# Output projection in two parts: groups B and C multiplied beside group A's attention and parked in DRAM, groups A and D after it

## The chip, the cores and the metric

The kernel runs on one core of one Trainium2 chip. The metric is the device time of one launch in microseconds, as the median of several runs. Lower is better. One further execution was recorded by the hardware profiler; the rows below come from it.

## The reference, cut to what matters

Two layers over 512 latent tokens and 256 context tokens, width 1024, float32. In each layer four head groups (A windowed attention, B convolution, C differential attention, D neighbourhood attention) each produce 256 of the 1024 channels. Their concatenation is multiplied by one matrix, gated and added to the stream; a normalisation that is scaled and shifted by the conditioning vector, and a feed-forward network, follow.

```python
y_a = window_gqa(qa, ka, va, ka_c, va_c, sink)
y_b = conformer_conv(ub, conv_w, conv_b, conv_ln_g, conv_ln_b)
y_c = diff_out(diff_attention_latent(qc, kc, vc, kc_c, vc_c, lam), subln_g, lambda_init)
y_d = neighbourhood_attn(qd, kd, vd, kd_c, vd_c, rpb)
yx = jnp.concatenate([y_a, y_b, y_c, y_d], axis=-1) @ w_out
...
x = x + g1 * yx
x = x + g2 * swiglu(modulate(rmsnorm(x, norm2_g[l]), sh2, sc2), w_gate[l], w_up[l], w_down[l])
```

The product can be cut along the channels: `[B C] @ w_out[256:768] + [A D] @ (the other 512 rows)` is the same sum. In the first layer the context tokens pass through the same steps; in the second only the latent tokens do.

## The kernel before, in words

Tokens are handled in row tiles of 128: tiles 0 to 3 are latent, 4 and 5 context. Layer 0 has six tiles, layer 1 four. Every float32 product of a weight and an activation is made of three matmuls on rounded parts (`mm3`, lines 174 to 179: high by high, high by low, low by high), so each operand is first split into a high part by ScalarE (line 142) and a low part by VectorE (line 144). Group outputs lie transposed in four tiles `yA` to `yD` (`self.yg`), two blocks of 128 channels each.

A layer (`layer`, line 995) is a sequence of stages. Inside a stage two generators run abreast: `beside(main, side, nm, ns)` (line 928) takes `ns` steps of the side work for every `nm` steps of the main work, which sets the order in which instructions are written down. A compile-time list scheduler takes that order as priority: on each engine, the earliest-written instruction that its model of the chip has ready goes next. After compilation the order on each engine and on SP's DMA queue is fixed, and each of them waits in order.

The stages around the change:

- Group D's second half, `beside(self.d_attn(l, ..., 1), rest(), dn, ...)` (line 1134). `rest` (line 1110) finishes group A's input projection, frees the input `hT`, opens the pool `wo` for the output weights, and runs `c_norm` (line 678), which normalises group C's output in pairs of row tiles through the PSUM tag `pu`.
- Group A's attention (line 1138): `a_attn` for two heads at a time, four query blocks each, and in layer 0 `ctx_attn` for the context tokens. Each block makes scores in the PSUM tag `sc`, a softmax on VectorE, ScalarE and GpSimd, transposes through `pt` (`tr_copy`, line 508), and the product with the values through `pu` (`pv`, line 616). Its side work is `more` (line 1119): it loads and splits output weights (`load_wo`, line 957; blocks 0 to 5 of 8 in layer 0, 0 and 1 in layer 1) and in layer 0 computes modulation vector 2 (`ada_gen`, `ada_half`, lines 335 and 298).
- The output projection (from line 1146). It reloads `x` (lines 1150 to 1155), loads the remaining output weights, loads and splits the first three feed-forward weights ahead, loads the gate `g1`, and then, row tile by row tile (context tiles first), splits the four groups into `yh` and `yl`, makes 8 blocks x 2 halves x 3 = 48 matmuls, and calls `add_gated` (line 981: one product `gt` from PSUM, line 984, and one sum into `x`, line 987) and for the first tiles `norm_rows` (line 362). In layer 0 modulation vector 4 is computed between the tiles: eight loads of 512 KB through `wraw` (3 buffers) and `araw` (1 buffer) in turn (`ada_load`, line 284), each followed by its matmuls (line 311), and a transpose per half (line 326). The second normalisation's scale is that vector. Before the last row tile's last blocks, `norm_mod` (line 394) transposes and modulates the first pair of normalised tiles; the feed-forward matmuls read its result.

PSUM has eight banks of 512 floats. Modes are pushed and popped as a stack (`PSUM_TAGS`, line 75): `t` holds `pt` (2 banks), `u` holds `pu` (2), and above them lies `c` (`sc`, 4 banks) or, in group D's stage, `e` (`sd` 2, `ptd` 2). So in group A's stage `sc` stands where `sd` and `ptd` stood, and `pu` keeps its banks.

## Time and profile before

| | |
|---|---|
| median of 3 runs | 1773.85 us (1773.67 to 1779.73) |
| the profiled execution's own time | 1774.57 us |
| its span, first to last instruction | 1772.7 us |
| TensorE matmul (PE) busy | 1701.2 us, 96% |
| weight load (PEld) busy, overlaps PE | 1412.6 us, 80% |
| VectorE (DVE), ScalarE (ACT), GpSimd (POOL) busy | 933.1, 583.3, 209.1 us |
| DMA | 172.78 MB, mean 97 GB/s |
| the chain that ended last | PE 84%, DVE 5%, DMA 4%, ACT 2% |

A row of a timeline gives start, duration, engine, line, operation, what it writes and reads, and in brackets the idle time of the engine before it and what ended that. A row of a windows view gives the length of a stretch, each engine's busy time with its instruction count, the clock granted to TensorE as a share of full speed, the share of time that the DMA engines were busy, and their GB/s. Matmuls are pipelined, so the distance between two starts, not the duration of one, is what a matmul costs.

### The profile page before, as it was taken

How to read it: one execution, taken by the hardware profiler on the slowest of the kernel's cores; microseconds unless marked ns; L12 is line 12 of the kernel's file. 1: busy time of each engine (PE TensorE's matmuls, PEld its weight loads, DVE VectorE, ACT ScalarE, POOL GpSimd, SP SyncE). 2: the span in 40 equal slices, each digit the busy share in tenths (PEclk: the TensorE clock that was granted, in tenths of full speed). 3: DMA queues.
4: the chain of work that ended last, by engine and by line, in shares of the span. 5: the costliest groups of instructions: out<-in, count | busy, mean ns of one | idle time of the engine just before them, and what ended most of it. 6: DMA issues, size and time to landing. Idle time of an engine off the chain costs nothing.

```text
span 1772.7 us, 27001 instructions
## 1 busy us (share of the span) xinstructions
PE 1701.2 (96%) x11236; PEld 1412.6 (80%) x11236; DVE 933.1 (53%) x1548; ACT 583.3 (33%) x1048; POOL 209.1 (12%) x194
## 2 busy tenths in 40 slices
PE   6999998889999999999999999999999999999997
PEld 4888777667888888888888888878767888888886
DVE  4678885663442343332333358688566545354354
ACT  4225553562241112121121224455365422321221
POOL 1101124330000010000000010112341001000000
PEclk8999999999999999999999999999999999999999
DMA  9351121325066344243221222211105253432421
GB/s 326 81 170 37 37 55 41 102 89 202 26 186 201 109 134 144 74 144 97 60 73 47 84 72 60 60 39 42 33 25 179 81 170 96 119 94 73 119 72 48
DMA packets 187976, 172.78 MB, mean 97 GB/s; under 512 B 17878, under 2 KB 150478, under 8 KB 187726
## 3 DMA queue, kind: packets, MB, share of 16 engines
q1 hardware_dynamic: 187854, 171.06, 31.6%
q8 instruction: 88, 1.44, 0.3%
q14 instruction: 34, 0.28, 0.0%
HBM read 166.76 MB, written 4.52 MB: 97 GB/s over the span
## 4 chain that ended last, share of the span: by engine, by line
PE 84%; DVE 5%; DMA 4%; ACT 2%; issue 1%; SPq 1%; POOL 1%; POOLq 0%; DVEq 0%; ACTq 0%
PE ps L177 19%; PE ps L178 19%; PE ps L179 19%; PE pu L177 5%; PE pu L178 5%; PE pu L179 4%; PE sc L630 3%; PE pt L515 3%; PE pt L621 2%; PE ada L311 2%; DMA wraw<-in_w_in 1%; SPq L98 1%; PE pu L621 1%; DMA x<-in_x 1%; DVE PT L529 1%
## 5 line engine op out<-in xcount | busy, mean ns | idle before, releaser
L178 PE MATMUL ps<-h,whi 128*128 128x512 f32 (+1 forms) x1104 | 382.8, 347 | 2.5 <-DVE h L144 2.5
L177 PE MATMUL ps<-h,whi 128*128 128x512 f32 (+1 forms) x1104 | 382.4, 349 | 0.9 <-DVE gt L984 0.9
L179 PE MATMUL ps<-h,wlo 128*128 128x512 f32 (+1 forms) x1104 | 381.6, 346 | 0.0
L142 ACT CAST whi<-wraw 128x1024 fp32r<-128x1024 f32 (+1 forms) x132 | 134.4, 1022 | 452.5 <-PE ps L178 248.8
L144 DVE TENSOR_TENSOR wlo<-wraw,whi 128x1024 fp32r<-128x1024 f32 (+1 forms) x116 | 137.7, 1190 | 193.5 <-ACT whi L142 192.4
L178 PEld LDWEIGHTS ps<-h,whi 128*128 128x128 f32 x1104 | 209.0, 189 | 29.1 <-DVE h L144 3.2
L177 PEld LDWEIGHTS ps<-h,whi 128*128 128x128 f32 x1104 | 207.8, 189 | 30.0 <-issue 2.4
L179 PEld LDWEIGHTS ps<-h,wlo 128*128 128x128 f32 x1104 | 208.9, 189 | 26.2 <-issue 0.4
L177 PE MATMUL ps<-wdhi,zh 128*128 128x512 f32 x440 | 171.6, 392 | 0.4 <-ACT ntmp L386 0.4
L178 PE MATMUL ps<-wdlo,zh 128*128 128x512 f32 x440 | 171.2, 390 | 0.0
L179 PE MATMUL ps<-wdhi,zl 128*128 128x512 f32 x440 | 170.6, 391 | 0.0
L177 PE MATMUL pu<-hT,whi 128*128 128x512 f32 (+1 forms) x456 | 161.1, 354 | 4.9 <-DVE V L910 3.8
L178 PE MATMUL pu<-hT,whi 128*128 128x512 f32 (+1 forms) x456 | 160.3, 352 | 0.0
L179 PE MATMUL pu<-hT,wlo 128*128 128x512 f32 (+1 forms) x456 | 159.7, 350 | 0.5 <-DVE wlo L144 0.5
L984 DVE TENSOR_TENSOR gt<-ps,g 128x1024 f32<-128x1024 f32 x66 | 80.7, 1223 | 134.2 <-PE ps L179 128.0
L142 ACT CAST wdhi<-wraw 128x1024 fp32r<-128x1024 f32 x44 | 46.1, 1052 | 272.6 <-PE ps L179 182.3
L987 POOL TENSOR_TENSOR x<-x,gt 128x1024 f32<-128x1024 f32 x12 | 29.7, 2474 | 728.7 <-DVE gt L984 728.7
L1250 DVE TENSOR_TENSOR sg<-sg,ps 128x768 f32<-128x768 f32 (+1 forms) x44 | 36.1, 821 | 145.8 <-PE ps L179 144.3
L879 DVE SCALAR_TENSOR_TENSOR accd<-hp,wcol,accd 128x783 f32<-128x783 f32 (+1 forms) x116 | 107.8, 929 | 2.7 <-ACT accd L875 1.2
L177 PEld LDWEIGHTS pu<-hT,whi 128*128 128x128 f32 x456 | 86.4, 190 | 20.2 <-DVE V L910 4.2
L177 PEld LDWEIGHTS ps<-wdhi,zh 128*128 128x128 f32 x440 | 82.6, 188 | 18.9 <-issue 1.0
L179 PEld LDWEIGHTS ps<-wdhi,zl 128*128 128x128 f32 x440 | 82.6, 188 | 17.8 <-issue 0.6
(260 smaller groups left out, 2712.3 us busy)
## 6 DMA issues: line engine op xcount, KB each, us to landing
araw<-in_w_ada SPq DMA_DIRECT2D x68, 512.0 KB
wraw<-in_w_gate SPq DMA_DIRECT2D x44, 512.0 KB
wraw<-in_w_up SPq DMA_DIRECT2D x44, 512.0 KB
wraw<-in_w_down SPq DMA_DIRECT2D x44, 512.0 KB
wraw<-in_w_in SPq DMA_DIRECT2D x40, 512.0 KB
wraw<-in_w_ada SPq DMA_DIRECT2D x17, 512.0 KB
wraw<-in_w_out SPq DMA_DIRECT2D x12, 512.0 KB
x<-in_x SPq DMA_DIRECT2D x8, 512.0 KB
```

The lines of the kernel that those rows point to most:

```text
L142: nc.scalar.copy(hi, src)
L144: eng.tensor_tensor(lo, src, f32(hi), op=ALU.subtract)
L177: mm(out, st[0], mv[0], start=first, stop=False)
L178: mm(out, st[0], mv[1], start=False, stop=False)
L179: mm(out, st[1], mv[0], start=False, stop=last)
L311: nc.tensor.matmul(ps[32 * j:32 * j + 32, 0:P], self.cstat[:, k, :], raw[:, a * 512 + j * P:a * 512 + (j + 1) * P], start=(k == 0), stop=( ...
L515: self.nc.tensor.transpose(pt[:, (i - a) * P:(i - a + 1) * P], blocks[i], self.ident)
L621: self.burst_of([lambda i=i, j=j: nc.tensor.matmul(po[64 * j:64 * j + 64, 0:P], *parts[j][i], start=(i == n - 1), stop=(i == 0)) for i in ...
L630: return [lambda o=o, q=q[a][r], k=k[b][r], i=i: self.nc.tensor.matmul(o, q, k, start=(i == 0), stop=(i == 2)) for i, (a, b) in enumerate( ...
L879: nc.vector.scalar_tensor_tensor(acc[:, 0:w], hp[:, k:k + w], wc, acc[:, 0:w], op0=ALU.mult, op1=ALU.add)
L984: nc.vector.tensor_tensor(tmp, ps, g, op=ALU.mult)
L1250: nc.vector.tensor_tensor(sg, sg, pss[1][:, 0:W], op=ALU.mult)
```

## The change

The four channel blocks 2 to 5 (groups B and C) of each row tile are multiplied in group A's stage, by a new generator `out_part`, copied from PSUM by ScalarE into an SBUF tile, and written to a DRAM tile `opark`. The later projection multiplies blocks 0, 1, 6, 7 only, loads the parked tile into `part`, and VectorE adds it before `add_gated`. Weight blocks 2 to 5 are loaded in `rest`, blocks 0 and 1 in `more`, blocks 6 and 7 afterwards, in both layers. Group A's stage gets a PSUM mode of its own, `a`: `sc` with 4 banks, `pu` with one and `pq` with one (the new product's, and the modulation's); mode `u` is popped for it, so `sc` now covers the two banks of the old `pu` and those of `sd`. The steps of side work per main work are changed with it, and in `norm_mod`'s place the condition `k == wa` becomes `k == 2` of four blocks.

```diff
+        "a": {"sc": (2048, 1), "pu": (512, 1), "pq": (512, 1)},
...
+        self.opark = self.tl(self.drp, [6, P, D], "opark")
...
+    def out_part(self, l, wo, pool, c2, order):
+
+        for n, i in enumerate(order):
+            yh, yl = (self.tl(pool, [P, 512], "rt", 4).bitcast(F32R).rearrange("p (k t) -> p k t", k=4) for _ in range(2))
+            for gi, gn in enumerate("BC"):
+                self.split(yh[:, 2 * gi:2 * gi + 2, :], yl[:, 2 * gi:2 * gi + 2, :], self.yg[gn][:, :, i * P:(i + 1) * P])
+            y = self.tl(pool, [P, 6, 256], "V", 1) if n % 2 else self.tl(c2, [P, 6, 256], "VD", 1)
+            y = y.rearrange("p a c -> p (a c)")[:, 0:D]
+            for hf in range(2):
+                c = slice(hf * 512, hf * 512 + 512)
+                ps = self.ps("pq")
+                for k in range(2, 6):
+                    self.mm3(ps, (yh[:, k - 2, :], yl[:, k - 2, :]), (wo[k][0][:, c], wo[k][1][:, c]), k == 2, k == 5)
+                nc = self.nc
+                nc.scalar.copy(y[:, c], ps)
+                if hf:
+                    self.dma(self.opark[i], y)
+                yield
...
             yield from self.c_norm(l, c1)
+            yield from self.load_wo(l, wo, held["wop"], range(2, 6))
 
         def more():
-            self.burst, self.ada_tag = 15, ("pu", "pt")[l]
+            self.burst, self.ada_tag = 15, "pq"
             self.atags = [("wraw", 3, F32, self.wst), ("whi", 3, F32R, self.wst), ("wlo", 3, F32R, self.wst)]
-            yield from self.load_wo(l, wo, held["wop"], range(wa))
+            yield from self.out_part(l, wo, c1, held["c2"], tiles)
+            yield from self.load_wo(l, wo, held["wop"], range(2))
             yield from self.ada_gen([] if l else [(0, 2)])
...
-        self.beside(self.d_attn(l, held["c2"], 1), rest(), dn, 4 if cx else 3)
+        self.beside(self.d_attn(l, held["c2"], 1), rest(), dn, 8 if cx else 7)
         self.psum_pop()
-        self.psum_push("c")
+        self.psum_pop()
+        self.psum_push("a")
         self.pv_tag = "pu"
-        self.beside(self.chain(self.a_attn(l, 0), self.a_attn(l, 1)), more(), 2 * dn, (12, 3)[l])
+        prs = order if cx else order[1:]
+        tiles = [i for pr in prs for i in pr]
+        self.beside(self.chain(self.a_attn(l, 0), self.a_attn(l, 1)), more(), 2 * dn, (16, 10)[l])
...
-        for _ in self.load_wo(l, wo, wop2, range(wa, NK)):
+        for _ in self.load_wo(l, wo, wop2, range(6, NK)):
...
-                yh = self.tl(op, [P, NK, P], "yh", 2, F32R)
-                yl = self.tl(op, [P, NK, P], "yl", 2, F32R)
-                for gi, gn in enumerate("ABCD"):
+                yh = self.tl(op, [P, 4, P], "yh", 2, F32R)
+                yl = self.tl(op, [P, 4, P], "yl", 2, F32R)
+                part = self.tl(op, [P, D], "part", 2)
+                self.dma(part, self.opark[i])
+                for gi, gn in enumerate("AD"):
...
-                for k in range(NK):
-                    if i == 3 and k == wa:
+                for k in range(4):
+                    if i == 3 and k == 2:
...
-                self.add_gated(xs[i], ps, g1[int(i >= 4)], op)
+                nc.vector.tensor_tensor(part, ps, part, op=ALU.add)
+                self.add_gated(xs[i], part, g1[int(i >= 4)], op)
```

## Rows read from the trace of the kernel before

**Rows 1.** The page, busy time of each engine and its share of the span

```profile
PE 1701.2 (96%) x11236; PEld 1412.6 (80%) x11236; DVE 933.1 (53%) x1548; ACT 583.3 (33%) x1048; POOL 209.1 (12%) x194
```

**Rows 2.** Windows, layer 0: group A's stage, its parts, and the output projection

```profile
345.00:402.00 57.00, 48.21 (x547) 36.51 (x543) 35.75 (x107) 35.40 (x96) 20.68 (x17) 0.94 0.27 86
...
360.00:380.00 20.00, 19.32 (x262) 14.77 (x262) 11.90 (x42) 10.58 (x34) 5.71 (x6) 1.00 0.16 55
380.00:390.00 10.00, 6.19 (x76) 4.76 (x76) 5.52 (x15) 5.63 (x12) 3.64 (x4) 1.00 0.29 82
390.00:402.00 12.00, 10.38 (x85) 7.41 (x85) 8.47 (x18) 8.02 (x25) 1.84 (x1) 0.72 0.77 246
...
402.00:474.00 72.00, 71.91 (x419) 58.30 (x418) 25.76 (x49) 13.04 (x33) 1.66 (x3) 1.00 0.38 127
```

**Rows 3.** Windows, layer 1: group A's stage, and the output projection

```profile
1302.00:1345.00 43.00, 38.36 (x364) 28.82 (x362) 27.00 (x82) 29.00 (x71) 20.22 (x18) 0.96 0.14 46
1345.00:1391.00 46.00, 45.44 (x207) 37.49 (x208) 22.78 (x37) 15.49 (x32) 1.66 (x3) 1.00 0.51 160
```

**Rows 4.** PE's timeline in layer 0's projection: two matmuls, 48 apart

```profile
404.05 0.39 PE L179 MATMUL ps<-wohi,yl 128*128 128x512 f32 x1
...
414.93 0.39 PE L179 MATMUL ps<-wohi,yl 128*128 128x512 f32 x1
```

**Rows 5.** PE's timeline at the end of layer 0's group A stage

```profile
384.59 0.98 PE L630 MATMUL sc<-qk,qk 64*128 64x256 f32 x12
388.75 0.63 PE L515 MATMUL pt<-ident,Pm 128*128 128x128 f32 x4 [3.19 <-DVE r L820]
...
393.62 2.39 PE L621 MATMUL pu<-PT,VA 128*64 128x128 f32 x18 [1.05 <-ACT PT L526]
```

**Rows 6.** DVE's timeline at the end of layer 1's group A stage

```profile
1335.99 3.81 DVE L144 TENSOR_TENSOR wolo<-wraw,wohi 128x1024 fp32r<-128x1024 f32 x3
```

**Rows 7.** ACT's copy of 512 columns from PSUM, in its timeline

```profile
398.11 0.59 ACT L526 COPY PT<-pt 128x512 f32<-128x512 f32 x1 [1.16 <-PE pt L515]
```

**Rows 8.** PE's timeline, layer 0: group C's norm and group A's first scores

```profile
324.29 0.60 PE L689 MATMUL pu<-ident,yC 128*128 128x128 f32 x4
...
345.45 0.96 PE L630 MATMUL sc<-qk,qk 64*128 64x256 f32 x12
...
353.37 0.66 PE L707 MATMUL pu<-ident,rt 128*128 128x128 f32 x4 [0.58 <-DVE rt L701]
```

**Rows 9.** PE's timeline, layer 0's projection: modulation vector 4, first modulated pair, first feed-forward matmuls

```profile
420.46 0.65 PE L311 MATMUL ada<-araw,cstat 128*32 128x128 f32 x16
...
443.14 0.64 PE L311 MATMUL ada<-araw,cstat 128*32 128x128 f32 x16
448.66 0.27 PE L326 MATMUL ada<-ident,adab 128*128 128x128 f32 x1
...
469.68 1.03 PE L381 MATMUL ada<-ident,xn 128*128 128x128 f32 x8
...
474.08 0.48 PE L177 MATMUL ps<-h,whi 128*128 128x256 f32 x2
```

**Rows 10.** SP's timeline, layer 0's projection: loads of the single buffer araw

```profile
407.08 0.75 SPq L98 DMA_DIRECT2D araw<-in_w_ada  x1
...
435.53 0.52 SPq L98 DMA_DIRECT2D araw<-in_w_ada  x1
```

**Rows 11.** Windows: the DMA engines as layer 0's projection begins

```profile
395.00:413.00 18.00, 17.77 (x116) 13.81 (x113) 6.25 (x19) 6.37 (x20) 0.00 (x0) 0.94 0.86 298
```

**Rows 12.** Tiles gt and yl, with DVE's timeline for xn: VectorE's durations in the projection

```profile
L984 DVE TENSOR_TENSOR gt<-ps,g x66: 1204/1225/1227, 415.6 to 1697.4; 128x1024 f32<-128x1024 f32 x66
L987 DVE TENSOR_TENSOR x<-x,gt x54: 1215/1225/2172, 416.9 to 1698.6; 128x1024 f32<-128x1024 f32 x54
...
L144 DVE TENSOR_TENSOR yl<-yA,yh x10: 416/418/426, 402.1 to 1369.1; 128x256 fp32r<-128x256 f32 x10
...
1363.48 0.75 DVE L368 TENSOR_SCALAR xn<-x,rs 128x1024 f32<-128x1024 f32 x1 [0.67 <-POOL rs L122]
```

More of the change, by code (lines that the diff above doesn't have):

```diff
@@ L969, in load_wo @@
             self.split(hi, lo, raw)
-            wo.append((hi, lo))
+            wo[k] = (hi, lo)
             yield 1.0
@@ L1091, in layer @@
         held = {}
-        wo, wa = [], (6, 2)[l]
+        wo = {}
         nq = 6 if cx else 4
@@ L1141, in layer @@
         c1.release()
-        self.psum_pop()
         self.psum_pop()
@@ L1167, in layer @@
         rows = []
-        prs = order if cx else order[1:]
         for pr in prs:
             for i in pr:
-                yh = self.tl(op, [P, NK, P], "yh", 2, F32R)
-                yl = self.tl(op, [P, NK, P], "yl", 2, F32R)
-                for gi, gn in enumerate("ABCD"):
+                yh = self.tl(op, [P, 4, P], "yh", 2, F32R)
[3 more added lines that the diff above has]
+                for gi, gn in enumerate("AD"):
                     self.split(yh[:, 2 * gi:2 * gi + 2, :], yl[:, 2 * gi:2 * gi + 2, :],
@@ L1183, in layer @@
                         c = slice(hf * 512, hf * 512 + 512)
-                        self.mm3(ps[:, c], (yh[:, k, :], yl[:, k, :]), (wo[k][0][:, c], wo[k][1][:, c]),
-                                 k == 0, k == NK - 1)
-                self.add_gated(xs[i], ps, g1[int(i >= 4)], op)
+                        self.mm3(ps[:, c], (yh[:, k, :], yl[:, k, :]), [a[:, c] for a in wo[(0, 1, 6, 7)[k]]],
+                                 k == 0, k == 3)
+                nc.vector.tensor_tensor(part, ps, part, op=ALU.add)
+                self.add_gated(xs[i], part, g1[int(i >= 4)], op)
                 if len(rows) < self.nxn:
```

## The prediction, made before the changed kernel was run

> **What bounds the kernel now.** I read the busy times first. TensorE is busy 96% of the span and no other engine over half [rows 1]; 1772.7 - 1701.2 = 71.5 us is all the visible idle time there is. The change removes no matmul; it can win only by moving matmuls into holes. So the second view is the windows of the stages that give and take. In layer 0, group A's stage has 57.00 - 48.21 = 8.8 us of PE idle, the projection after it 0.1 us in 72; in layer 1 the stage has 43.00 - 38.36 = 4.6 us, the projection 0.6 us [rows 2, 3]. The holes are not spread evenly: of the 8.8 us, (10.00 - 6.19) + (12.00 - 10.38) = 5.4 us lie after 380, and between 360 and 380 PE is busy 19.32 of 20 us [rows 2]. PE's timeline shows the end: the last scores are issued at 384.59, then PE waits 3.19 us for one softmax, and a product of 18 matmuls takes 2.39 us [rows 5], in a stretch whose granted clock was 0.72 [rows 2]. That is one block's chain through four engines with nothing beside it.
>
> **What moves.** Two matmuls 48 apart in the projection start 10.88 us apart, 0.227 us each [rows 4]. The moved half is 6 tiles x 24 x 0.227 = 32.7 us in layer 0 and 4 x 24 x 0.227 = 21.8 us in layer 1. These leave the projections and enter group A's stages; unless they fill holes the sum is nought.
>
> **Group A's stage, layer 0: -3.5 us.** The side steps are written at 16 for every 20 of the attention, the 12 of the projection first, so these end at the fifteenth attention step of 20. The scheduler follows that order, so I let them fill the 3.4 us before the tail (8.8 - 5.4) [rows 2], and leave the tail, as its fill is the two output weight blocks and the modulation vector. Bounds: 0, if the new waits eat it, and -12 us if the tail fills too: the 8.8 us, and the clock's loss, 12 us at 0.72 instead of 1.00, which is 3.4 us. The added work on other engines lies beside PE: per row tile two ScalarE copies of 0.59 us [rows 7] and two splits of 0.42 us on VectorE [rows 12], 6 x (1.2 + 0.8) us, where VectorE and ScalarE are busy 36 and 35 of 57 us [rows 2]; if that cover went, it would cost up to 12 us. The ten writes of 512 KB to DRAM go out on SP while the DMA engines are 27% and 14% busy [rows 2, 3], and wait for ScalarE's copy. Behind each on SP's queue stand only weight loads that have the rest of the stage: nothing. The stage ends no earlier for them.
>
> **Group A's stage, layer 1: -5 us.** Here the side steps run to the end (10 for 16, eight of the projection). I take 3 of the 4.6 us [rows 3]. Another 2 us come from the weights: at the end of the stage VectorE works 3.81 us on three low parts [rows 6] and three more follow; now only blocks 6 and 7 come so late, so four of six splits leave the tail, of which I let half count. Bounds 0 and -7.
>
> **The start of group A's stage: +1 us.** The scores now stand where `pu` stood, so the first of them must wait for group C's norm, which ends its work in `pu`. Before, the norm began at 324.29 and sent its last transposes at 353.37, while the first scores were issued at 345.45 [rows 8]: kept as it is, the wait costs 8 us. But the norm is written twice as early in group D's stage now (8 side steps per 10 instead of 4), ahead of the weight splits that it shared VectorE with. Bounds -2 (the norm out of the way sooner) and +8; I take 1, since only the order of a few microseconds of work has to turn. Behind the waiting scores stand the whole of group A's chain, and the projection for tiles 4 and 5, which needs the norm's last pair.
>
> **The projection, layer 0: +10 us.** This is the term that decides. The feed-forward's first matmuls start at 474.08, 4.4 us after the transposes of the first pair at 469.68, and what these are modulated with is vector 4, done with its last transpose at 448.66 [rows 9]. Before, that vector was early by 21 us. Its matmuls were not paced by PE: four of the eight loads go through one buffer, used at 420.46 first and at 443.14 last, each load issued only after the use before it [rows 9], the first at 407.08, the last at 435.53 [rows 10]. The first was issued behind `x` and the gates, with the DMA engines 86% busy [rows 11]. None of that gets shorter by moving matmuls. The vector is ready 448.66 - 402 = 46.7 us after the stage begins, the feed-forward can start 4.4 us later at 51; PE's own work is now 72.1 - 32.7 = 39.4 us. The stall is 51 - 39.4 = 12 us, more with the parked tiles: six loads of 0.52 MB at 298 GB/s [rows 11] are 10.5 us of the DMA engines, two of them ahead of the first `araw` load, 3.5 us. Less, if the scheduler gives the vector's matmuls earlier places once PE is free: the first use at 414 instead of 420, as the DMA engines were done at 413 [rows 11], would leave 5. Bounds 0 and 15; I take 10, close to the chain's own row.
>
> **The projection, layer 1: +3.5 us.** There is no modulation vector. PE needs 24 x 0.227 = 5.46 us for a tile. VectorE needs for it the new sum, the product and the sum into `x`, 1.22 us each, two splits of 0.42 and the norm's 0.75 [rows 12]: 5.25 us, and the splits of the three weights ahead, about 1.2 us each, lie in the same 22 us: 24.6 us against 21.8. Before, it had 11 us per tile. Then the last tile's chain into the second norm is longer by one sum of 1.22 us. In sum 2.8 + 1.2 = 4 us, half a microsecond of which is the idle that it had already [rows 3]. Bounds 0 and 7. In layer 0 the same sums (6 x 1.22 us) lie under the vector's chain and cost nothing; if that chain proves short, they are the next to be late, at 0 to 3 us.
>
> **The sum.** -3.5 - 5 + 1 + 10 + 3.5 = +6 us on the profiled execution's own 1774.57, which is its span of 1772.7 and 1.9 around it: 1780.6. That execution stands 0.7 us above the median of the runs shown, so the forecast for the median is 1780.
>
> **A rule that speaks against it.** In group A's stage before, with short products through single banks and gaps of under a microsecond between them, the granted clock was 1.00 from 360 to 380; it fell to 0.72 only after waits of several microseconds [rows 2, 5]. The Trainium skill, TensorE: Matmul & The Clock Gate, section "A second HAM failure mode: psum-queue depth-cycling", says that a kernel whose matmul groups take turns in PSUM banks idles briefly between groups, and that the clock then swings between its two levels. By the row the single bank `pq` costs nothing in clock; by the rule the whole moved half would run at a lower one. This case's row speaks against it for attention's short groups, and no row shows it for groups of twelve.
>
> **Rivals.**
>
> *A: the vector keeps up.* For it: the DMA engines sit idle part of the time after 413, and PE's places for the vector's matmuls were chosen by the scheduler, not by the landing. Against it: one buffer, four loads in a row [rows 9, 10]. Without the +10 the time is 1770, and with the tails of both stages filled too (-12 and -7 instead of -3.5 and -5) 1759. Faster by 4 to 15 us.
>
> *B: the one-bank waits, slower.* `pu` and `pq` have one bank each, so PE can start the next half only after ScalarE's copy, and the next product with the values only after its own. Place: 12 + 8 halves; price at least the copy, 0.59 us [rows 7], when no other PE work is ready at that moment: 20 x 0.59 = 12 us, on top of the forecast 1792. It decides where the attention's operations are all waiting for their softmax at once, that is, when more than about half of the halves end in such a moment. For it: the tail in rows 5. Against it: PE has work from 360 to 380 at 97%.
>
> *C: the clock.* By the rule above as a mechanism here: 54.5 us of moved matmuls at 0.72 instead of 1.00 take 54.5 x 0.39 = 21 us more, 1801.
>
> *D: it does not do what it says.* The scheduler leaves the moved products to the end of the stage, where they stand alone: no hole is filled, the extra work stays: 1780 + 8.5 = 1789.
>
> **How the numbers follow.** A difference under 0.5%, 8.9 us, cannot be told from no change here, so the bounds are 1765 and 1782.7. Forecast: 0.46, its own range 1772 to 1788 by the bounds of the terms (0.02 of it faster, 0.30 within, 0.14 slower). A: 0.31 (0.14 faster, 0.17 within). B: 0.17 (0.02 within, 0.15 slower). C 0.04 and D 0.02, slower. So faster 0.16, within 0.49, slower 0.35. For 8 in 10 the range runs from 1762, which takes in most of A, to 1793, which takes in B and D.
>
> **What would show it.** In layer 0, PE idle just ahead of the first feed-forward matmuls, ended by the chain of vector 4, 5 to 15 us, with the `araw` uses still about 7 us apart; no such idle and A is right. In group A's stages, PE busy near 97% up to the tail, and the tail of layer 0 still there. In layer 1, VectorE without pauses in the projection. First scores at most a few microseconds after group C's last transposes. Idle after each twelve matmuls on `pq`, ended by ScalarE, would be B; a granted clock under 1.00 in the dense part, C. The forecast is wrong if the first feed-forward matmuls of layer 0 start within 42 us of the projection's first.

## The result, and the profile after

The changed kernel takes 1798.54 us (median of four runs, 1796.52 to 1799.65) against 1773.76 us for the kernel before: a ratio of 1.013, 95% interval 1.0109 to 1.015. It is slower, by 24.8 us where 6 were forecast, and lies 5.5 us above the range that the prediction gave 8 in 10. In the profiled executions the span goes from 1772.7 to 1796.2 us, by 23.5.

The page, busy time of each engine and its share of the span, after:

```profile
PE 1709.9 (95%) x11236; PEld 1417.4 (79%) x11236; DVE 948.8 (53%) x1558; ACT 595.5 (33%) x1068; POOL 212.5 (12%) x194
```

The matmuls are the same 11236 as in [rows 1]. TensorE's busy time grew by 8.7 us, so some 15 us of the loss are new idle time. Where it lies is read from windows cut at events in TensorE's timeline: group C's first normalization transposes, group A's first scores, the projection's first matmul, the feed-forward's first, and in layer 0 the first product with w_down. The columns are start:end, length, then busy time (instructions) of PE, PEld, DVE, ACT and POOL, the granted clock, the DMA engines' share and GB/s. The kernel before, layer 0 and layer 1:

```profile
324.30:345.50 21.20, 15.90 (x131) 12.49 (x130) 16.13 (x35) 13.38 (x30) 7.28 (x4) 0.84 0.52 161
345.50:402.10 56.60, 47.73 (x542) 36.19 (x541) 35.74 (x107) 35.23 (x95) 20.68 (x17) 0.94 0.27 86
402.10:474.10 72.00, 72.00 (x419) 58.39 (x419) 25.84 (x49) 12.94 (x32) 1.66 (x3) 1.00 0.38 127
474.10:556.30 82.20, 80.87 (x716) 71.74 (x714) 35.39 (x46) 31.11 (x40) 2.83 (x3) 1.00 0.57 174
...
1283.90:1302.30 18.40, 15.68 (x145) 11.65 (x143) 13.63 (x31) 11.41 (x25) 7.38 (x6) 0.91 0.19 58
1302.30:1345.40 43.10, 38.06 (x361) 28.69 (x360) 27.10 (x82) 29.11 (x71) 20.22 (x18) 0.96 0.15 49
1345.40:1391.40 46.00, 45.84 (x209) 37.76 (x210) 22.38 (x37) 15.34 (x30) 1.66 (x3) 1.00 0.51 160
```

The changed kernel, the same stretches:

```profile
323.80:351.30 27.50, 16.33 (x145) 12.56 (x143) 18.43 (x40) 16.02 (x38) 7.96 (x5) 0.92 0.43 125
351.30:430.70 79.40, 76.82 (x656) 59.66 (x656) 37.36 (x111) 42.28 (x111) 18.09 (x16) 0.96 0.19 66
430.70:481.60 50.90, 44.15 (x290) 34.68 (x290) 33.33 (x48) 11.49 (x23) 3.48 (x3) 0.88 0.81 288
481.60:568.40 86.80, 83.18 (x714) 73.28 (x714) 34.08 (x43) 30.76 (x40) 1.92 (x3) 0.97 0.54 172
...
1295.30:1328.40 33.10, 21.98 (x171) 16.04 (x169) 23.05 (x46) 20.55 (x41) 9.46 (x8) 0.85 0.48 128
1328.40:1386.10 57.70, 55.74 (x430) 42.21 (x429) 26.54 (x79) 31.31 (x75) 18.26 (x16) 1.00 0.20 68
1386.10:1414.40 28.30, 24.79 (x113) 20.41 (x113) 18.30 (x27) 7.79 (x16) 4.42 (x3) 0.95 0.66 234
```

Subtract PE's busy time from the length, line by line. In group A's two stages the holes go from 8.9 + 5.0 to 2.6 + 2.0 us: the change does what it says there, 9.4 us of holes are gone. But ahead of group A they grow from 5.3 + 2.7 to 11.2 + 11.1 us (+14.3), in the projections from 0.0 + 0.2 to 6.8 + 3.5 (+10.1), behind layer 0's projection from 1.3 to 3.6 (+2.3). The busy time of the seven stretches together grows by 6.9 us for the same matmuls (2523 and 2519 records); the granted clock is higher in group A's stages (0.96 and 1.00 for 0.94 and 0.96) and lower in the projections and behind layer 0's (0.88, 0.95 and 0.97 for 1.00). The sum, -9.4 + 14.3 + 10.1 + 2.3 + 6.9 = 24.2, is the loss, within a microsecond of the 23.5 by which the span grew.

The largest new hole is ahead of group A in layer 1. VectorE's timeline there, after (start, us, instruction, and in brackets the idle time ahead of it and what ended it; the changed kernel's line numbers are one or two above those of the kernel before):

```profile
1297.32 3.49 DVE L145 TENSOR_TENSOR wolo<-wraw,wohi 128x1024 fp32r<-128x1024 f32 x3
1300.72 0.69 DVE L806 CUSTOM_DVE_ANT_1 Pm<-sd,dnb 128x512 f32<-128x512 f32 x1
...
1301.33 0.68 DVE L695 TENSOR_REDUCE ss<-rt 128x8 f32<-128x512 f32 x1
1301.93 0.68 DVE L531 COPY PT<-pt 128x512 f32<-128x512 f32 x1
...
1303.41 1.24 DVE L145 TENSOR_TENSOR wolo<-wraw,wohi 128x1024 fp32r<-128x1024 f32 x1
...
1306.80 1.23 DVE L145 TENSOR_TENSOR wolo<-wraw,wohi 128x1024 fp32r<-128x1024 f32 x1 [2.07 <-ACT wohi L143]
...
1309.61 1.23 DVE L145 TENSOR_TENSOR wolo<-wraw,wohi 128x1024 fp32r<-128x1024 f32 x1 [0.92 <-ACT wohi L143]
```

and TensorE's in the same stretch:

```profile
1296.86 0.97 PE L795 MATMUL sd<-qk,qk 64*128 64x256 f32 x12
...
1302.66 1.97 PE L623 MATMUL pt<-PT,VD 128*64 128x128 f32 x14 [2.33 <-DVE PT L531]
...
1309.80 2.08 PE L479 MATMUL pt<-rt,perm 128*128 128x512 f32 x2 [3.13 <-ACT yD L628]
...
1316.69 1.09 PE L623 MATMUL pt<-PT,VD 128*64 128x128 f32 x14 [1.81 <-ACT PT L528]
```

Group D's scores `sd` were issued at 1296.86, but VectorE had three splits of output weights in its queue (`wolo`, the subtraction of `split`), and reached the scores at 1300.72, group C's norm (the sum `ss`, line 695) at 1301.33 and the copy of the transposed probabilities at 1301.93; TensorE's product waited 2.33 us for it. All six splits of the weight pool lie in this half of group D now; the kernel before had two there in layer 1:

```profile
1285.92 2.35 DVE L144 TENSOR_TENSOR wolo<-wraw,wohi 128x1024 fp32r<-128x1024 f32 x2
```

In layer 0 the wait stands elsewhere. TensorE's timeline, after, at group A's first scores:

```profile
349.73 0.77 PE L709 MATMUL pu<-ident,rt 128*128 128x128 f32 x4 [4.55 <-DVE rt L703]
351.28 1.65 PE L632 MATMUL sc<-qk,qk 64*128 64x256 f32 x12 [0.78 <-ACT yC L711]
```

The first scores come right behind group C's last normalization transposes and the ScalarE step that empties them. Before, they were issued 7.9 us ahead of those transposes [rows 8]: that wait comes with the banks.

The end of layer 0's projection, after: TensorE, the loads of `araw` on SP's queue, and two windows:

```profile
468.82 0.62 PE L313 MATMUL ada<-araw,cstat 128*32 128x128 f32 x16
...
475.63 1.08 PE L313 MATMUL ada<-araw,cstat 128*32 128x128 f32 x16 [5.75 <-DMA araw<-in_w_ada]
477.12 0.48 PE L328 MATMUL ada<-ident,adab 128*128 128x128 f32 x1 [0.41 <-DVE adab L318]
...
481.62 0.58 PE L178 MATMUL ps<-h,whi 128*128 128x256 f32 x1
```

```profile
454.84 0.42 SPq L99 DMA_DIRECT2D araw<-in_w_ada  x1
464.93 0.38 SPq L99 DMA_DIRECT2D araw<-in_w_ada  x1
469.66 0.53 SPq L99 DMA_DIRECT2D araw<-in_w_ada  x1
```

```profile
460.00:470.00 10.00, 9.88 (x98) 7.53 (x97) 9.47 (x11) 1.15 (x2) 2.93 (x2) 1.00 0.65 229
470.00:484.00 14.00, 6.78 (x38) 5.09 (x39) 9.10 (x17) 4.61 (x8) 0.48 (x1) 0.61 0.60 199
```

This is the chain that the prediction named: the last load of vector 4 went out at 469.66, behind the use of its buffer at 468.82, TensorE waited 5.75 us for it, and the granted clock of the window with this wait was 0.61. Before, the same buffer was last used at 443.14 [rows 9].

### The profile page after: what moved, and what is told of

Read it like the earlier page. It is cut to its first block, busy times and chain, and to the rows that moved or that the text cites. A ratio compares the mean times of both kernels' runs of the same rounds, so it can differ in the third digit from the quotient of the medians.

```text
span 1796.2 us, 27095 instructions
## 1 busy us (share of the span) xinstructions
PE 1709.9 (95%) x11236; PEld 1417.4 (79%) x11236; DVE 948.8 (53%) x1558; ACT 595.5 (33%) x1068; POOL 212.5 (12%) x194
## 4 chain that ended last, share of the span: by engine, by line
PE 84%; DVE 6%; DMA 5%; ACT 2%; issue 1%; SPq 1%; POOL 1%; POOLq 0%; DVEq 0%; ACTq 0%
PE ps L178 17%; PE ps L179 17%; PE ps L180 17%; PE pu L178 5%; PE pu L179 5%; PE pu L180 5%; PE sc L632 3%; PE pt L517 3%; PE pt L623 2%; PE ada L313 2%; SPq L99 1%; PE pq L178 1%; DMA araw<-in_w_ada 1%; PE pu L623 1%; PE pq L180 1%
## 5 line engine op out<-in xcount | busy, mean ns | idle before, releaser
L1005 DVE TENSOR_TENSOR gt<-ps,g 128x1024 f32<-128x1024 f32 x56 | 68.4, 1223 | 100.7 <-PE ps L180 95.2
L180 PEld LDWEIGHTS pu<-hT,wlo 128*128 128x128 f32 x456 | 86.8, 190 | 13.0 <-issue 1.4
```

The costliest lines, as they stand in the source:

```text
L180: mm(out, st[1], mv[0], start=False, stop=last)
L1005: nc.vector.tensor_tensor(tmp, ps, g, op=ALU.mult)
```

## Experiments

Sixteen kernels were run, each with its stage lengths read at the same events as above: "start" is group C's first normalization transposes to group A's first scores, "A" from there to the projection, "proj" from there to the feed-forward, "ffn" in layer 0 from there to the first w_down product (us). The ratio is to the kernel before on the same chip, with its 95% interval; the kernel before took 1773.8 to 1776.9 us on the chips used, so two rows are compared by their ratios.

| kernel | median us | ratio | l0 start, A, proj, ffn | l1 start, A, proj |
|---|---|---|---|---|
| before | 1773.76 | 1 | 21.2, 56.7, 72.0, 82.2 | 18.4, 43.1, 46.0 |
| after | 1798.54 | 1.013 [1.0109, 1.015] | 27.5, 79.4, 50.9, 86.8 | 33.1, 57.6, 28.3 |
| e1 banks kept | 1792.41 | 1.0094 [1.0079, 1.0109] | 21.9, 81.6, 52.7, 87.9 | 28.1, 61.2, 27.5 |
| e2 weights later | 1798.63 | 1.0125 [1.011, 1.014] | 29.2, 77.4, 53.0, 85.2 | 31.5, 57.3, 27.7 |
| e4 vector 4 early | 1795.89 | 1.0108 [1.0092, 1.0125] | 30.0, 82.7, 44.1, 87.5 | 31.5, 57.7, 28.1 |
| b1 banks only | 1783.5 | 1.0042 [1.0027, 1.0057] | 26.9, 56.3, 73.5, 82.2 | 20.2, 43.4, 48.2 |
| b2 splits only | 1781.7 | 1.0039 [1.0025, 1.0053] | 21.5, 57.7, 72.0, 83.6 | 24.3, 42.6, 45.6 |
| e6 splits held | 1794.22 | 1.0104 [1.0079, 1.0128] | 21.1, 87.8, 56.0, 84.5 | 17.9, 64.6, 28.2 |
| e7 banks kept, splits held | 1787.76 | 1.0069 [1.0054, 1.0084] | 13.6, 88.4, 54.5, 84.4 | 16.7, 67.1, 27.9 |
| e7 in layer 1 alone | 1780.39 | 1.0036 [1.0023, 1.0049] | 22.1, 56.4, 72.0, 84.2 | 16.7, 67.0, 28.0 |
| e8 two araw | 1790.73 | 1.0082 [1.0067, 1.0097] | 13.6, 87.4, 50.3, 87.2 | 16.7, 67.5, 31.0 |
| e9 splits on GpSimd | 1785.47 | 1.0049 [1.0032, 1.0066] | 21.7, 81.0, 51.5, 83.7 | 21.2, 62.7, 27.3 |
| e10 both | 1792.95 | 1.0091 [1.0075, 1.0106] | 21.3, 81.3, 50.4, 90.6 | 21.8, 62.6, 31.1 |
| change in layer 1 alone | 1785.1 | 1.0052 [1.0037, 1.0066] | 21.1, 56.4, 72.0, 82.5 | 31.0, 57.6, 28.2 |
| e11 two araw, two part | 1784.47 | 1.0046 [1.0033, 1.006] | 13.6, 87.7, 49.6, 88.0 | 16.7, 67.5, 28.0 |
| e12 no parked load | 1782.92 | 1.0045 [1.0028, 1.0061] | 13.6, 87.9, 55.6, 83.4 | 16.7, 67.0, 25.1 |
| e13 no load, two araw | 1781.51 | 1.0036 [1.0023, 1.0049] | 13.6, 87.7, 55.6, 84.2 | 16.7, 66.9, 24.9 |
| e14 before, splits held | 1773.49 | 0.9997 [0.9984, 1.0009] | 13.6, 64.8, 72.0, 81.9 | 15.6, 43.5, 46.0 |

Two theories stood at the start: T1, the late start of group A comes from the banks (the scores stand where `pu` stood and wait for group C's norm); T2, it comes from the weight splits beside group D.

**e1, the banks as before.** The parked product uses the pair of `pu`, in the pool "c" of before.

```diff
-                ps = self.ps("pq")
+                ps = self.ps("pu")
...
-            self.burst, self.ada_tag = 15, "pq"
+            self.burst, self.ada_tag = 15, "pu"
...
-        self.psum_pop()
-        self.psum_push("a")
+        self.psum_push("c")
...
+        self.psum_pop()
```

> The changed kernel, with the PSUM banks of group A's stage as they were before: the scores over sd and ptd, pu with its two banks, shared by the products with the values, the parked half of the projection and modulation vector 2. Theory T1 (banks: group A's first scores wait for group C's norm, since they now stand on pu): the late start of group A's stage goes, 7.3 us in layer 0 and 14.7 us in layer 1, so 1776 to 1780 us, and in the trace the first scores of layer 1 come before the last products of group D again. Theory T2 (splits: the four weight blocks that are split beside group D's second half hold VectorE and ScalarE, and group D and the norm end later): the start stays late in layer 1, 1790 to 1798 us.

Measured 1792.41, in T2's range. Layer 0's start is back at the kernel before's, 21.9 for 21.2; layer 1's is not, 28.1 for 18.4. The banks are nearly all of layer 0's late start (5.6 of 6.4 us) and a third of layer 1's (5.0 of 14.7).

**e2, the weights asked for later.** The paces of the side steps beside groups D and A are set to match.

```diff
             yield from self.c_norm(l, c1)
-            yield from self.load_wo(l, wo, held["wop"], range(2, 6))
...
+            yield from self.load_wo(l, wo, held["wop"], range(2, 6))
             yield from self.out_part(l, wo, c1, held["c2"], tiles)
```

> The changed kernel, with weight blocks 2 to 5 loaded and split at the head of group A's side work instead of at the end of group D's, so that they come after group D's operations in the scheduler's order; the PSUM banks stay as in the changed kernel. T1 (banks): the start of group A's stage stays late, 1795 to 1802 us, perhaps a little more, since the parked half must wait for its weights. T2 (splits): group D's second half in layer 1 ends about 14 us sooner, and 1782 to 1788 us.

Measured 1798.63. This told nothing on T2: although they are written later, the splits still stand in group D's second half in the trace (from 1298.41 on), for the scheduler put them there. It does show that the pace of the side steps is not the cause: at 4 and 3 in place of 8 and 7, layer 1's start is still 31.5 us (33.1).

**e4, vector 4 moved beside group A.**

```diff
-            yield from self.ada_gen([] if l else [(0, 2)])
+            yield from self.ada_gen([] if l else [(0, 2), (0, 4)])
...
-        adas = self.ada_gen([(0, 4)] if l == 0 else [])
+        adas = self.ada_gen([])
```

> The changed kernel, with modulation vector 4 of layer 0 computed as the last side work of group A's stage (behind vector 2, its eight loads through the nine free weight buffers) instead of between the row tiles of the projection. If the loads through the single buffer araw set the end of layer 0's projection: PE's wait of 5.8 us for the last load and the cold stretch behind it go, first feed-forward matmuls about 40 us after the projection's first instead of 51, and 11 to 16 us less in all, 1782 to 1788 us. Rival: VectorE's sums and the parked tiles' DMA set the same end, then the first feed-forward matmuls come 47 to 50 us after the projection's first, 1794 to 1799 us.

Measured 1795.89. The feed-forward starts 44.1 us after the projection (50.9), so the chain was what made it late. But the start grows by 2.5 us, group A's stage pays 3.3 us for the vector, the feed-forward takes 0.7 longer, the projection still does not reach the 39.3 us that its matmuls had before, and the first w_down product comes at 568.44, where it was at 568.41.

**b1, the kernel before with the new banks alone.**

```diff
+        "a": {"sc": (2048, 1), "pu": (512, 1), "pq": (512, 1)},
...
-            self.burst, self.ada_tag = 15, ("pu", "pt")[l]
+            self.burst, self.ada_tag = 15, "pq"
...
-        self.psum_push("c")
+        self.psum_pop()
+        self.psum_push("a")
...
-        self.psum_pop()
```

> The kernel before, with nothing of the change but the PSUM mode of group A's stage: pu and pq with one bank each and the scores over the old pu. T1 (banks): the first scores of both layers wait for group C's norm, 8 us in layer 0 (last transposes of the norm at 353.4 against first scores at 345.5) and 2 to 4 us in layer 1, where the norm ended 1 us after the first scores: 1780 to 1788 us. T2 (splits): within 3 us of the kernel before, 1771 to 1777 us.

Measured 1783.5, as T1 has it: layer 0 starts group A 5.7 us later. Layer 1's group A starts only 1.8 later. The two projections are 1.5 and 2.2 us longer without any new wait of TensorE, at a granted clock of 0.98 and 0.95 in place of 1.00.

**b2, the kernel before with the splits alone**, and the paces set to match.

```diff
             yield from self.c_norm(l, c1)
+            yield from self.load_wo(l, wo, held["wop"], range(2, 6))
...
-            yield from self.load_wo(l, wo, held["wop"], range(wa))
+            yield from self.load_wo(l, wo, held["wop"], range(2))
```

> The kernel before, and of the change only the weight blocks 2 to 5 in group D's second half: no parked product, the banks as before. T2 (the splits): group D's second half in layer 1, 25.2 us from the first normalization transposes of group C to D's last product before, grows to 37 to 39 as in the changed kernel, group A starts late, and the time is 1782 to 1790. T1 (the banks): that stage stays at 25 to 27 and the time is 1772 to 1777. If both are true each has a part: 1777 to 1782.

Measured 1781.7: each has a part. Layer 1's start grows by 5.9 us, layer 0's by 0.3. In layer 1 b1 and b2 make 7.7 of the 14.7 us; the other 7.0 come only in combination. The banks cost 1.8 alone and 5.0 with the rest of the change (after against e1), the splits 5.9 alone and 9.7 with the parked product (e1); why is not shown. Layer 0 could not show more, since the kernel before had its six splits there already. VectorE's timeline, before, layer 0:

```profile
323.82 2.35 DVE L144 TENSOR_TENSOR wolo<-wraw,wohi 128x1024 fp32r<-128x1024 f32 x2
...
334.12 1.23 DVE L144 TENSOR_TENSOR wolo<-wraw,wohi 128x1024 fp32r<-128x1024 f32 x1 [0.34 <-ACT wohi L142]
```

**e6, the splits really held.** In the changed kernel the splits of blocks 2 to 5 are ordered, on ScalarE and VectorE, behind group A's first softmax instructions (`afirst`), with the paces of e2.

```diff
-            yield from self.load_wo(l, wo, held["wop"], range(2, 6))
...
+            yield from self.load_wo(l, wo, held["wop"], range(2, 6), self.afirst)
             yield from self.out_part(l, wo, c1, held["c2"], tiles)
...
-            self.split(hi, lo, raw)
+            with contextlib.ExitStack() as es:
+                for s in hold:
+                    es.enter_context(self.tc.issue_after(s.ins))
+                self.split(hi, lo, raw)
```

> The changed kernel with the four splits of weight blocks 2 to 5 held, on ScalarE and VectorE, behind group A's first softmax instructions. T2: group D's second half in layer 1 goes back to 25 to 28 us (39 in the changed kernel), group A's first scores come 9 to 12 us sooner, and the time is 1785 to 1791. T1 (the banks alone): D's stage stays long or the scores stay late, 1795 to 1800. A third way: the work held back slows group A's stage by as much as D's stage gains, since the parked product's first tile waits for it: 1793 to 1799 with a stage A over 63 us in layer 1 (57.6 in the changed kernel).

Measured 1794.22, the third way. T2 holds for the start: layer 1's falls from 33.1 to 17.9 us. But group A's stages take 64.6 and 87.8 us in place of 57.6 and 79.4: half in layer 1, and more than all in layer 0, is given back.

**e7, banks kept and splits held.** The edits of e1 and e6 together.

> Both held splits and the banks of before (parked product on the bank pair of pu, no new pool). If banks and splits are two separate costs, this takes both away: layer 1's group A starts within 4 us of the kernel before (7 to 8 us after group C's last normalization), and the time is 1779 to 1786, what is left being layer 0's projection (+10 to +16) less what group A's stages give (-7 to -17). If the banks' part is only a second name for the splits' delay, it equals the run with the splits held alone, within 2 us.

Measured 1787.76, 10.8 us under the change, still over the kernel before and 1.8 over what was expected. The start in layer 1 is now 1.7 us shorter than before, so banks and splits explain the late start in full. Its windows in layer 1, start and stage A, and TensorE's timeline as the stage begins:

```profile
1291.80:1308.50 16.70, 14.92 (x149) 11.22 (x147) 12.20 (x33) 11.49 (x30) 8.73 (x7) 1.00 0.01 1
1308.50:1375.60 67.10, 59.37 (x454) 45.74 (x453) 38.98 (x92) 40.24 (x87) 19.64 (x18) 0.95 0.39 118
```

```profile
1308.47 0.98 PE L632 MATMUL sc<-qk,qk 64*128 64x256 f32 x12
...
1330.12 0.50 PE L178 MATMUL pu<-wohi,rt 128*128 128x512 f32 x1
```

The parked product, which is to fill the holes of group A, starts 21.7 us into the stage: VectorE works on the weights' splits up to 1326.5; the holes of the stage are 7.7 us, more than the 5.0 before. Splits ahead of group A delay its start, splits behind it delay its filler.

**e7 in layer 1 alone**, layer 0 as before.

```diff
+        nw = l == 1
...
+            if nw:
+                yield from self.load_wo(l, wo, held["wop"], range(2, 6), self.afirst)
+                yield from self.out_part(l, wo, c1, held["c2"], tiles)
```

> As the run with banks kept and splits held, but the change is made in layer 1 alone; layer 0 is as before. Layer 0's cost in the projection (11.6 us and 4.6 behind it) and its gain in the stage of group A (9.9) both go. By the sum: layer 1's stage A -7, its projection +4, its start 0 to +4: 1772 to 1778, no difference from the kernel before, or 3 us under it. If layer 1's start stays 10 us late whatever is done with banks and splits: 1782 to 1787.

Measured 1780.39, above the first range and under the second, though the start is 1.7 us short of before. The miss is stage A: 67.0 us where 43.1 + 21.8 = 64.9 would be the moved matmuls on top, so nothing of the expected 7 us was left. Layer 1's change then still costs 5.6 us (ratio 1.0036).

**The change in layer 1 alone**, as it is.

```diff
+        nw = l == 1
...
+            if nw:
+                yield from self.load_wo(l, wo, held["wop"], range(2, 6))
...
-        self.psum_push("a")
+        self.psum_push("a" if nw else "c")
```

> The change as it is, made in layer 1 alone (layer 0 as before). By the sum over the traces layer 1 costs +14.7 at the start of group A, -7.3 in its stage, +4.1 in the projection, +0.6 behind it: 12 us over the kernel before, 1786 to 1788. If the layers do not add (layer 0's change moves layer 1's queues): under 1783 or over 1791.

Measured 1785.1, a microsecond under the range. But the kernel before took 1776.93 on this chip, so layer 1's change costs 8.2 us by the medians (interval 6.6 to 11.7) where the sum had 12; its start is 31.0 for 33.1 us. Whether the layers add is not shown, since layer 0 was not changed alone.

**e9, the subtractions on GpSimd.** e1, with:

```diff
-            self.split(hi, lo, raw)
+            self.split(hi, lo, raw, None, 2 <= k < 6)
```

> Banks kept, weight blocks 2 to 5 split in group D's second half as in the change, but their subtractions on GpSimd (the casts stay on ScalarE). If VectorE's queue was what the splits held up: layer 1's D stage, from group C's first normalization transposes to A's first scores, goes from 28 (banks kept) to 17 to 21 us, stage A stays at 57 to 61, and the time is 1781 to 1786, under the run with held splits since the parked product can start with group A. If GpSimd (which normalizes every softmax) or ScalarE takes VectorE's place as the one that is late: the D stage stays over 24 us and the time is 1788 to 1794.

Measured 1785.47 against e1's 1792.41 (ratio 1.0049 for 1.0094). Layer 1's start falls from 28.1 to 21.2 us though the splits stay in group D's half, at the same paces and with the same banks: VectorE's queue was what they held up. Of e1's 9.7 us, 2.8 remain. Stage A is 62.7 us, over the 57 to 61 expected. GpSimd's timeline in layer 1:

```profile
1293.71 7.54 POOL L145 TENSOR_TENSOR wolo<-wraw,wohi 128x1024 fp32r<-128x1024 f32 x3 [2.97 <-ACT wohi L143]
```

**e8, two buffers for vector 4.** e7, with:

```diff
-                part = self.tl(op, [P, D], "part", 2)
+                part = self.tl(op, [P, D], "part", 1)
...
-        self.ada_tag, self.burst, self.atags = "ada", 0, [("wraw", 3, F32, self.wst), ("araw", 1, F32, op)]
+        self.ada_tag, self.burst, self.atags = "ada", 0, [("wraw", 3, F32, self.wst), ("araw", 2, F32, op)]
```

> As the run with banks kept and splits held, and in the output projection two buffers for modulation vector 4's weights in place of one, paid for with one buffer in place of two for the parked tile. If the chain of vector 4 through its single buffer sets the end of layer 0's projection: from the projection's first matmul to the first of the FFN 54.6 us go to 44 to 48, and the time to 1778 to 1783. If the transfers as a whole (x, weights, parked tiles, vector 4: DMA share 0.84 in this stretch) or VectorE set it: 51 to 56 us, and 1785 to 1790.

Measured 1790.73, by the ratios not faster than e7. The feed-forward starts 50.3 us after the projection for 54.5, in neither range, but is 2.8 longer itself, and layer 1, which has no vector 4, loses 3.0 us in its projection to the single parked buffer.

**e10, e8's edit on e9.**

> Both: subtractions on GpSimd and two buffers for vector 4. If the two costs are separate, the gains of both add: 1772 to 1779, at most as fast as the kernel before. If one of the two earlier runs misses, this follows the other.

Measured 1792.95, a miss: as in e8 the single parked buffer costs layer 1 3.8 us (31.1 for 27.3), and layer 0's feed-forward takes 6.8 longer.

**e11, two buffers for vector 4, both for the parked tile.** e7, paid for in layer 0 with one buffer for `yh` and one for `yl`:

```diff
-                yh = self.tl(op, [P, 4, P], "yh", 2, F32R)
-                yl = self.tl(op, [P, 4, P], "yl", 2, F32R)
+                yh = self.tl(op, [P, 4, P], "yh", 1 if cx else 2, F32R)
+                yl = self.tl(op, [P, 4, P], "yl", 1 if cx else 2, F32R)
...
-        self.ada_tag, self.burst, self.atags = "ada", 0, [("wraw", 3, F32, self.wst), ("araw", 1, F32, op)]
+        self.ada_tag, self.burst, self.atags = "ada", 0, [("wraw", 3, F32, self.wst), ("araw", 2 if cx else 1, F32, op)]
```

> As the run with banks kept and splits held; in layer 0's projection vector 4 has two buffers and the parked tile keeps its two, paid for with one buffer in place of two for the split tiles yh and yl; layer 1 as it was. If vector 4's chain through one buffer is what layer 0's projection lost: the FFN starts 44 to 48 us after the projection's first matmul (54.6 with one buffer, 50.3 with two but a single parked tile), and the time is 1778 to 1783. If the sum of the transfers is the limit: 50 to 55 us, 1784 to 1789.

Measured 1784.47. 4.9 us are gained up to the feed-forward, which starts after 49.6 us, in neither range, and 3.7 of them are lost again up to w_down. The waits for `araw`, 4.9 us in e7, are gone from the projection. Where TensorE is idle now, VectorE is busy 9.46 of 10 us, as e11's window shows:

```profile
465.00:475.00 10.00, 6.83 (x35) 5.09 (x34) 9.46 (x14) 4.21 (x8) 0.40 (x1) 0.90 0.56 197
```

The loss behind it is no wait. The stretch from the feed-forward's first matmul to w_down, e7 and then e11:

```profile
480.50:564.80 84.30, 81.39 (x713) 71.56 (x714) 33.53 (x43) 30.69 (x40) 2.09 (x3) 1.00 0.56 177
...
473.00:561.00 88.00, 85.57 (x713) 75.48 (x714) 33.75 (x43) 30.76 (x40) 2.13 (x3) 0.94 0.53 164
```

TensorE's idle time there is 2.9 us in e7 and 2.4 in e11. Its busy time grew by 4.2 us for the same matmuls, at a granted clock of 0.94 for 1.00; the first ten of e11's were at 0.66.

**e12, no parked load, and e13, with two buffers for vector 4 as well.** e7, with:

```diff
-                part = self.tl(op, [P, D], "part", 2)
-                self.dma(part, self.opark[i])
...
-                nc.vector.tensor_tensor(part, ps, part, op=ALU.add)
-                self.add_gated(xs[i], part, g1[int(i >= 4)], op)
+                self.add_gated(xs[i], ps, g1[int(i >= 4)], op)
```

Both leave the part of groups B and C out of the sum, to see what bringing it back costs.

> As the run with banks kept and splits held, but the projection neither loads the parked tiles nor adds them, so the part of groups B and C is missing from the output; vector 4 keeps its one buffer. If the transfers (5.2 MB of parked tiles in both layers) or VectorE's sums set the end: layer 0's FFN starts 44 to 49 us after the projection's first matmul, layer 1's 25 to 26 us (27.9), and the time is 1775 to 1781. If vector 4's chain sets it: 51 to 55 us in layer 0 all the same, 1783 to 1787.

> Both: no parked loads or sums (the part of groups B and C is missing from the output), and two buffers for vector 4. If the chain and the transfers are together all that layer 0's projection lost, PE has nothing left to wait for: 44 to 46 us, which is the busy time of PE in that stretch, and the time is 1772 to 1778. If it stays over 49 us, something else (VectorE's normalizations, x) sets it.

Measured 1782.92 and 1781.51. In layer 1 it is clean: 25.1 us for 27.9, so the parked tiles' loads and sums cost 2.8 us there. In layer 0 both leave 55.6 us, which was not expected of e13. TensorE's waits in layer 0's projection, e12 (total us, times, longest):

```profile
PE ada L313 <- DMA araw<-in_w_ada: 5.9, 1, 5.9
PE ps L178 <- DVE gt L1010: 4.0, 1, 4.0
```

and e13:

```profile
PE ps L178 <- DVE gt L1010: 5.7, 1, 5.7
PE ada L313 <- DMA araw<-in_w_ada: 3.4, 2, 1.7
```

Leaving out the sum made a wait of its own: the sum had emptied the PSUM tile, and without it the tile is held until the product with the gate, and VectorE waited for the gate's load (1.1 us in e12, 3.3 in e13). How much of layer 0's wait is the parked tiles' transfers therefore stays open.

**e14, the kernel before with its own splits held** behind group A's first softmax, as in e6.

```diff
-            yield from self.load_wo(l, wo, held["wop"], range(wa))
+            yield from self.load_wo(l, wo, held["wop"], range(wa), self.afirst)
```

> The kernel before, nothing parked, the banks as before; only its own splits of output weight blocks beside group A (six in layer 0, two in layer 1), which its trace shows within group D's second half, are held behind group A's first softmax instructions. If T2 holds for the kernel before as well: layer 0's group A starts 6 to 8 us sooner (21.2 us after group C's first normalization transposes before, 13 to 15 expected), stage A gives back 1 to 4 of it, and the time is 1768 to 1773, under both kernels. If all of it is given back in stage A: 1773 to 1777.

Measured 1773.49 against 1774.84: no difference, the second way. Group A starts 7.5 us sooner in layer 0, and its stage is 8.1 us longer. Its windows at the stage's beginning show why:

```profile
337.00:347.00 10.00, 5.72 (x56) 4.61 (x53) 7.66 (x17) 8.38 (x17) 3.72 (x2) 0.95 0.24 59
347.00:357.00 10.00, 7.34 (x45) 5.45 (x43) 7.91 (x16) 5.91 (x11) 7.91 (x5) 0.54 0.67 210
```

Group A alone leaves TensorE 4.3 us idle in ten, and in the next ten the granted clock was 0.54. Over the whole stage 4.5 us more are idle and 3.7 more busy than before. None of the versions is measurably faster than the kernel before.

## Why the prediction was wrong

**The step that failed: "The start of group A's stage: +1 us".** It measured +6.4 us in layer 0 and +14.7 in layer 1, by the start column. It failed in two ways. The prediction saw the wait for group C's norm and its price of 8 us, and then took 1, trusting that the norm, written twice as early and ahead of the splits, would be out of the way. It was not: in layer 1's rows above the first three splits (1297.32) stand in VectorE's queue ahead of it (1301.33), and in layer 0 5.6 to 5.7 us of the banks' wait are paid (e1, b1), inside the bound of 8 that stood there. In layer 1 the step was not costed at all; the 1 rests on layer 0's rows alone. The prediction counted the four splits that leave the end of group A's stage as a gain of 2 us, and put no price on the place where they go: the half of group D in which VectorE normalizes scores for a TensorE that has little else. b2 gives them 5.9 us alone; with the banks kept, taking them off VectorE gives back 6.9 (e1 28.1, e9 21.2), and holding them, with other paces and the two splits that stood there before held too, 11.4 (e7 16.7). Its first reading already missed this engine: it has no engine but TensorE over half busy, where [rows 1] has VectorE at 53%. That a start can be made good again in the stage behind it (e14) is no defence for layer 1: start and stage A together came to +14.7 - 7.3 = +7.4 us where the prediction had -5. In layer 0 they came to +6.4 - 9.9 = -3.5, where it had -2.5. Of the 17.5 us between the 6 of the sum and the 23.5 of the spans, 12.4 are layer 1's start and stage, and 4.6 lie behind layer 0's projection.

**Group A's stages, -3.5 and -5: borne out in layer 0, not in layer 1.** Stage lengths less the moved 32.7 and 21.8 us changed by -9.9 and -7.3. In layer 0 the tail filled too, as the upper bound had it: 2.6 us of idle time are left in the stage. But e14 shows that start and stage trade, so the two have to be read together. In layer 0 they make 77.8 us before, and less the moved work 74.3 after, 69.3 in e7 and 70.1 in e9: some 8 us were filled. In layer 1 they make 61.5 before, 69.0 after, and 60.7 to 62.2 in e6, e7 and e9: where the start is made good the stage's gain is gone. Part of why is in the windows: the changed kernel has 171 matmuls ahead of group A for 145, and 430 in its stage where 361 + 96 would be 457, since matmuls of groups C and D that came behind group A's first scores now come ahead of them. The 3 us of holes that the prediction counted on in layer 1 were not gained.

**Layer 0's projection, +10: right in its time and in the last wait.** It measured 50.9 us, where 51 was worked out, 11.6 more than the moved matmuls left: 6.8 as idle time and 4.8 as busy time at the lower clock, which the prediction had not counted. Vector 4's last transpose came 46.4 us into the stage, for 46.7. The wait is in the rows, vector 4 through one buffer, and e4 and e11 take it away. The steps before it match less well, so the closeness is in part luck: the first three uses of `araw` (454.13, 464.23 and 468.82) waited for no load, as none of the four did before, so TensorE's own order set them, 10.1, 4.6 and 6.8 us apart where about 7 was expected. What the prediction missed is what comes next: with that wait gone, e4 pays for it at the start and in group A's stage, and e11 as clock behind the projection. It also ended the account at the feed-forward's first matmul; 4.6 us more were lost behind it, half as idle time and half as busy time at a clock of 0.97.

**Layer 1's projection, +3.5: right in number, the mechanism only in part.** It measured +4.1, and e12 puts 2.8 of it on the parked tiles' loads and sums. But the prediction took VectorE to be full, 24.6 us of work against 21.8, and expected it without pauses; it was busy 18.3 of 28.3 us. It had to wait for the first parked tile, 11 us into the stage, with the DMA engines over 90% busy in the first ten of them, which that term did not have, and its steps crowd behind that. TensorE's new waits, 3.5 us, lie at the end, at the norm's transposes. VectorE and TensorE there, after:

```profile
1397.19 1.22 DVE L1212 TENSOR_TENSOR part<-ps,part 128x1024 f32<-128x1024 f32 x1 [3.90 <-DMA part<-opark]
...
1412.76 1.97 PE L383 MATMUL ada<-ident,xn 128*128 128x128 f32 x8 [2.44 <-ACT ntmp L388]
```

**The rivals.** B did not occur: no wait of TensorE in group A's stages ends in the copy out of `pq`, and the copies took 0.58 us beside other work. C did not occur. The granted clock of the changed kernel at the beginning of layer 0's stage and in the dense stretches of layer 0 and layer 1:

```profile
351.30:360.00 8.70, 8.70 (x46) 7.02 (x47) 3.66 (x11) 3.33 (x9) 2.04 (x2) 0.68 0.01 2
360.00:380.00 20.00, 20.00 (x148) 15.74 (x147) 12.09 (x36) 12.52 (x35) 6.97 (x6) 1.00 0.13 53
...
1335.00:1380.00 45.00, 44.57 (x331) 33.64 (x328) 20.10 (x67) 25.48 (x60) 16.18 (x14) 1.00 0.12 48
```

The groups of twelve matmuls take turns on one bank there. The first 8.7 us, behind the waits at the stage's start (4.55 and 0.78 us in the rows above), were at 0.68; after them, with the same groups, the clock stays at its upper level. The section "A second HAM failure mode: psum-queue depth-cycling" of the Trainium skill (TensorE: Matmul & The Clock Gate) speaks of short idle times between the groups; here other matmuls stand between them and TensorE is busy 20.00 of 20 us, so the case that it describes did not arise. C's price, 1801, came near the time measured for another reason, which is luck. D did not occur either: the parked matmuls of layer 0 start at 352.86 and end at 416, well spread over a stage from 351.3 to 430.7. The sum by steps, against +6: -0.5 arrival, +6.4 and -9.9, +11.6, +4.6, -0.7 up to layer 1, +14.7 and -7.3, +4.1, +0.6, which is the 23.5 of the spans.

## What to carry to other kernels

Work that is moved into holes brings its operands with it: look for where their preparation lands, on which engine's queue, and who waits there, before the gain of the holes is counted. A stage that was full of TensorE's work may have been the cover of several chains at once, here a vector's loads, the parked tiles and VectorE's steps; when the cover goes, removing one of them can only show the next, as e11 did. And an order written in the code need not be the scheduler's: look in the trace where an instruction was put, and hold it by a dependency where that matters.

## What was not expected of the hardware

The cost of a stall went beyond its length. In the changed kernel the 5.75 us wait for `araw` lies in a window with a granted clock of 0.61, and in e14 ten microseconds with 4.3 idle were followed by ten at 0.54, in which TensorE was busy 7.34 us. In e11 the feed-forward has no more idle time than in e7 and is 3.7 us longer, at 0.94 for 1.00. Over the seven stretches 6.9 us of 24.2 are such time: busy time that the same matmuls took more. The prediction had counted holes, and the clock only in one stage's bound and in rival C.
